# A hybrid decoder layer in float32: the 512 moving columns of the wide matmuls taken in turns from their two halves

## The chip, the core and the metric

The kernel runs on one core of one Trainium2 chip. The metric is the device time of one execution in microseconds. TensorE is called PE below, its weight load PEld, VectorE DVE, ScalarE ACT, GpSimd POOL, and SyncE, which issues the transfers, SP.

## The reference

One layer on 256 tokens of width 2048: a SwiGLU half-step, a token mixer of two branches side by side, and a second SwiGLU half-step, each between two RMS norms.

```python
h = rmsnorm(x, ffn1_norm_pre)
x = x + 0.5 * rmsnorm(swiglu(h, w_gate, w_up, w_down), ffn1_norm_post)   # 2048 -> 5632 -> 2048
h = rmsnorm(x, mix_norm_pre)
proj = h @ w_in                                   # 2048 -> 13376 columns, split in nine
y_a = mla_branch(c_q, c_kv, k_rope, ...)          # latent attention, 16 heads, then @ mla_w_o
y_b = hgrn2_branch(hq, hf, hi, hg, ...)           # gated linear recurrence, 16 heads, then @ hgrn_w_o
y = (sigmoid(gate_a) * y_a + sigmoid(gate_b) * y_b) @ w_out
x = x + rmsnorm(y, mix_norm_post)
...                                               # and the second SwiGLU half-step as the first
def swiglu(h, w_gate, w_up, w_down):
    return (jax.nn.silu(h @ w_gate) * (h @ w_up)) @ w_down
```

Nearly all of the work is in these products of a [256, K] activation with a weight matrix, and all weights are read once.

## The kernel before

**Operands.** Every float32 operand of a large product is held as an exact sum of two float32r parts, called hi and lo. An activation lies in SBUF transposed, as [feature in 128 partitions, part, k-tile, token], so that for one k-tile the 256 columns of hi and the 256 columns of lo are two runs of 256 with a gap between them (`act(k)`, a view of 128 x 2 x 256). A weight tile of 128 x 1024 is loaded by SP into `raw` (L83, four buffers), copied to hi by ACT (L95) and subtracted by DVE to give lo (L96). The product leaves out lo times lo.

**Two shapes of product.** `gemm_t` makes 256 weight columns at a time, with the weights stationary. For each k-tile and each half of the 256 columns it issues two matmuls into one PSUM bank of 512 columns: the weights' lo with the 256 hi columns of the activation as moving columns (L114, which adds into columns 0 to 255 of the bank), and the weights' hi with all 512, hi and lo (L115, which adds into all 512). In the first k-tile the wide one comes first (L111, then L112). The two halves of the bank are added at the end (L120 and L121). `gemm_n` makes 512 weight columns, with the activation stationary and 512 weight columns moving, and issues three matmuls for each k-tile and each half of the tokens through `_tok`: L126 (activation hi, weight hi), L127 (activation hi, weight lo), L128 (activation lo, weight hi), all into the same 512 columns.

**Stages.** Each half-step computes its first 512 columns of gate and up with `gemm_n`, then twenty rounds of a gate product (L295, `pg`) and an up product (L299, `pu`) with `gemm_t`, and then the down product with `closing`, which calls `gemm_n` for three quarters of the columns (L238) and once more, in another order of the tokens, for the fourth. The mixer calls `gemm_t` for the two gates (`gate_a`, `gate_b`), for the two output projections (`mla_w_o` with the tile `oa`, `hgrn_w_o` with the tile `ob`), and for q and f of the recurrence; `w_out` is again a `closing`. Tiles are named by use: `h` and `after` are the normed activations, `at` the SwiGLU product, `mg` the merged branches; `whi` and `wlo` are the split weights, `wpair` the split weights of a pass that are kept for the second half of the tokens.

**Order.** Each engine runs a fixed list of instructions. PE's list has the two matmuls of `gemm_t` by turns and the three of `gemm_n` in a row, with few other things between them in the stages named here.

Of the kernel before, what the change touches and what calls it, by code (L numbers as in the profile page):

```python
# [19 lines left out]
P = 128  # L20
# [3 lines left out]
KD = D // P  # L24
# [13 lines left out]
# Where the next operand's transposes stand in program order, along the product that runs beside them (see gemm_n), and  # L38
# by how many instructions the rest of that operand's chain is put ahead; columns of the residual at a time.
# [9 lines left out]
def _two_pi_parts():  # L49
    """2 pi as a sum of four 12-bit numbers and a rest."""  # L50
    parts, rest = [], TWO_PI
    for _ in range(4):
        step = 2.0 ** (np.floor(np.log2(rest)) - 11)
        c = np.floor(rest / step) * step
        parts.append(float(c))
        rest -= c
    parts.append(float(np.float32(rest)))
    return parts


class Ops:
    """Pools and the pieces that the stages share."""
# [36 lines left out]
    def gemm_t(self, w, act, kt):  # L99
        """256 weight columns, result transposed: a bank for 128 columns, [column, token] in two addends."""  # L100
        nc = self.nc
        ps = self.mm.tile([P, 2, 512], F32, name="mm")
        for g in range(kt // 4):
            hi, lo = self.load_w(w[g])
            for i in range(4):
                k = g * 4 + i
                for j in range(2):
                    c = slice(i * 256 + j * P, i * 256 + (j + 1) * P)
                    both = act(k)
                    if k == 0:  # L110
                        nc.tensor.matmul(ps[:, j], hi[:, c], both, start=True, stop=False)  # L111
                        nc.tensor.matmul(ps[:, j, 0:T], lo[:, c], both[:, 0], start=False, stop=False)  # L112
                    else:
                        nc.tensor.matmul(ps[:, j, 0:T], lo[:, c], both[:, 0], start=False, stop=False)  # L114
                        nc.tensor.matmul(ps[:, j], hi[:, c], both, start=False, stop=k == kt - 1)  # L115
        return ps

    def total(self, out, ps):
        """The sum of gemm_t's two addends."""
        self.nc.scalar.copy(out=out, in_=ps[:, :, T:512])  # L120
        self.nc.vector.tensor_tensor(out=out, in0=out, in1=ps[:, :, 0:T], op=ALU.add)  # L121

    def _tok(self, ps, hi, lo, act, k, kt, i, n, tt):
        nc = self.nc
        r, c, both, o = slice(tt * P, (tt + 1) * P), slice(i * n, (i + 1) * n), act(k), ps[tt][:, 0:n]
        nc.tensor.matmul(o, both[:, 0, r], hi[:, c], start=k == 0, stop=False)  # L126
        nc.tensor.matmul(o, both[:, 0, r], lo[:, c], start=False, stop=False)  # L127
        nc.tensor.matmul(o, both[:, 1, r], hi[:, c], start=False, stop=k == kt - 1)  # L128

    def gemm_n(self, w, act, kt, n=512, late=0, pool=None, own=0, hooks=()):  # L130
        """n weight columns, result [token, column], a bank for each half of the tokens.

        The first half of the tokens ends its last `late` k-tiles before the second half starts them. Their
        weights are in `pool`, but for the first `own` tiles. `hooks` are functions to call at points that run
        from -1 to 0 along the first half of the tokens, and from 0 to 1 along the second's last k-tiles."""
        kg = 1024 // n
        banks = self.mm.tile([P, 2, 512], F32, name="mm")
        ps = [banks[:, 0], self.mm.tile([P, 2, 512], F32, name="mm")[:, 1] if late else banks[:, 1]]
        held = []
        hooks = list(hooks)  # L140

        def call(at):
            while hooks and hooks[0][0] <= at:
                hooks.pop(0)[1](ps)

        for g in range(kt // kg):
            hold = g * kg >= kt - late
            hi, lo = self.load_w(w[g], pool if hold and g * kg >= kt - late + own * kg else None)
            call(g * kg / kt - 1)
            for i in range(kg):  # L150
                k = g * kg + i
                self._tok(ps, hi, lo, act, k, kt, i, n, 0)
                if hold:
                    held.append((hi, lo, k, i))
                else:
                    self._tok(ps, hi, lo, act, k, kt, i, n, 1)
        for m, (hi, lo, k, i) in enumerate(held):
            call(m / len(held))
            self._tok(ps, hi, lo, act, k, kt, i, n, 1)
        call(1)  # L160
        return ps if late else banks
# [10 lines left out]
    def rstd_of(self, ssq, n, width, half=False):  # L172
        """ssq [P, n] sums of squares -> 1 / sqrt(mean + eps), or half of it."""
# [20 lines left out]
    def transposed(self, src, act, c, tt):  # L194
        """split(transpose(src)) into the k-tiles 4c.. of act."""
# [10 lines left out]
    def prenorm(self, x, ssq, wname, act, tt, ws=None):  # L206
        """act = split(transpose(x * rstd * w)) for half of the tokens."""
# [10 lines left out]
    def weighted(self, ps, c, z, wname):  # L218
        """z = y * w, a quarter of the columns."""
        w = self.bcast(wname, c)  # L220
        self.nc.vector.tensor_tensor(out=z[:, c * 512:(c + 1) * 512], in0=ps, in1=w, op=ALU.mult)

    def residual(self, x, z, rstd, done):
        """x += rstd * z, some of the columns at a time."""
# [6 lines left out]
    def closing(self, w, act, kt, late, own, pool, post, half, x_src, x_dst, nxt):  # L231
        """The last product of a stage, its norm, the residual, and the next stage's operand.

        Returns the hooks of the next product, which end the operand."""
        z = [pool.tile([P, D], F32, name=f"z{tt}") for tt in range(NT)]
        yssq = [self.ssq4() for _ in range(NT)]
        for c in range(3):
            ps = self.gemm_n(w[c], act, kt)  # L238
            for tt in range(NT):
                self.square_sum(yssq[tt][:, c:c + 1], ps[:, tt])  # L240
                self.weighted(ps[:, tt], c, z[tt], post)
# [26 lines left out]
def layer_kernel(ctx, tc, a, out):  # L268
# [9 lines left out]
    def ffn(n, act, fp, x_src, x_dst, nxt, hooks=()):  # L278
# [3 lines left out]
        # the first columns by halves of the tokens  # L282
# [8 lines left out]
        for c in range((FF - FF_N) // 256):  # L291
            pg = ops.gemm_t(wg[c], act, KD)
# [3 lines left out]
            pu = ops.gemm_t(wu[c], act, KD)  # L296
# [48 lines left out]
    def gate_b(c):  # L345
        pg = ops.gemm_t(a["w_gb"][c], h, KD)
# [8 lines left out]
    for c in range(8):  # L355
        py = ops.gemm_t(a["mla_w_o"][c], lambda k: oa[:, :, k, :], KD)
# [9 lines left out]
    with tc.tile_pool(name="mg", bufs=1, side="right", reuse_waits="tile") as mgp:  # L366
        mg = mgp.tile([P, 2, KD, T], F32R, name="mg")
        for c in range(8):
            if c < 6:
                gts.append(gate_b(c + 2))  # L370
            py = ops.gemm_t(a["hgrn_w_o"][c], lambda k: ob[:, :, k, :], KD)
# [19 lines left out]
def rope_tables(ops, pool):  # L391
    """cos and sin of positions * inv_freq as [token, half of the tokens, HALF]."""
# [17 lines left out]
    # whole turns off: their number in parts of ten bits, so that each product with a part of 2 pi is exact  # L410
# [22 lines left out]
def mla(ops, mp, c_q, hm, h, oa, gate):  # L433
# [16 lines left out]
    def rope(dst, src, tt, n):  # L450
        """src [P, n, 64] -> dst, rotated."""
# [18 lines left out]
    # k_rope: product transposed, back to [token, dim], rotated, transposed, for the even and the odd  # L470
    # head of a pair in its half of the partitions, with zeros in the other
# [52 lines left out]
    def scores(pair, qn, kn, v):  # L524
        """The weights of a pair of heads, and what is left to do with them."""
# [46 lines left out]
    # a pair's projections, the weights of the pair before, and the output of that one later on  # L572
# [26 lines left out]
def hgrn(ops, gp, h, ob, fill):  # L599
# [8 lines left out]
    # lower bound: first row of the softmax over the two rows of logits  # L608
# [14 lines left out]
    def pair_in(pr, step):  # L623
        """q, f, k as [feature, half of the tokens, head, token]; the second half runs back in time."""
# [28 lines left out]
    def values_in(g):  # L653
        """Values of four heads, [token, half of the tokens, head and feature]."""
# [5 lines left out]
    def gates_in(g):  # L660
        """Their output gates, with the norm's weights."""
# [11 lines left out]
    def scan(pr, q, f, k, four):  # L673
        """pre: products of f within blocks up to and with t; suf: products after s to the end of the block.

        Scores of pairs (s, t) in the two halves of a block of 2n tokens are k suf . q pre with blocks of n. In
        the second half of the tokens time runs back, so that there an earlier s has the place of a later
        one in the first half: one product gives both."""
# [7 lines left out]
        def part(t, n, early):  # L686
            """The earlier (or later) halves of the blocks of 2n: [P, half of the tokens, block, n]."""
# [3 lines left out]
        def ends(t, n, early):  # L691
            """The last element in time of those halves, over n columns."""
# [3 lines left out]
        def halves(t, n, tt, early):  # L696
            """The same as part, of one half of the tokens: [P, block, n]."""
# [93 lines left out]
    # a pair's products, the scores of the one before, and the output of the one before that  # L791
# [33 lines left out]
def _tiles(w, cols, group):  # L825
    """[K, C] -> [C / cols, K / (group * 128), 128, group * cols]"""
# [6 lines left out]
def _tokens(x):  # L833
    """Tokens in the kernel's order: the second half runs back in time."""
# [64 lines left out]
```

## Time and profile before

| | before |
|---|---|
| two timed runs, us | 2564.88 and 2566.22, median 2565.55 |
| the profiled execution's own time, first to last instruction, us | 2564.2 |
| PE busy, us | 2521.4 (98%) |
| weight loads busy, us | 2147.1 (84%) |
| DVE, ACT, POOL busy, us | 1477.7, 1186.9, 181.1 |
| mean granted TensorE clock | 0.999 |
| read from HBM, MB | 472.61 |

The profile has no other time of the profiled execution than its span, which is 1.35 us below the median of the timed runs. Matmuls overlap in the pipeline, and the end of each is modelled, so that a row's duration (393 ns for a matmul of 512 columns) is longer than the time that the matmul takes from its neighbours. What one matmul costs is read from the distance of the starts in the timeline.

### The profile page before, as it was taken

To read this page: it belongs to the slowest core of one execution; us is meant where nothing else is said; L and a number is where in the kernel's file an instruction comes from. 1 tells how busy PE (TensorE), PEld (TensorE's weight loads), DVE (VectorE), ACT (ScalarE), POOL (GpSimd) and SP (SyncE) were. 2 spreads that over 40 slices of the span, in tenths; PEclk is the share of its full clock that TensorE was granted. 3 is DMA by queue.
4 is the path that set the end of the run, shared out by engine and by line. 5 is a ranking of instruction groups with operands and counts; after the bars stand their busy time and mean duration, and the time that the engine had idled before them with its cause. 6 is when DMAs were issued, how large, how long until landed. Compare 5 with 4: busy or idle time off the path is not lost.

```text
span 2564.2 us, 33907 instructions
## 1 busy us (share of the span) xinstructions
PE 2521.4 (98%) x13316; PEld 2147.1 (84%) x13316; DVE 1477.7 (58%) x1732; ACT 1186.9 (46%) x1552; POOL 181.1 (7%) x181
## 2 busy tenths in 40 slices
PE   8999999999999999999999999999999999999998
PEld 6888888888878898888888888888788888888887
DVE  5555555544466666556777776555655555554444
ACT  5444444434344556444444444444544444443433
POOL 0000000000000100111323231120000000000000
PEclk9999999999999999999999999999999999999999
DMA  7555555556686444555545444567755555555655
GB/s 255 174 188 189 188 183 190 188 188 199 201 271 188 162 140 148 188 181 181 165 163 169 161 157 158 188 205 242 231 175 188 187 186 188 189 189 188 197 195 184
DMA packets 137248, 481.13 MB, mean 188 GB/s; under 512 B 15616, under 2 KB 16000, under 8 KB 136320
## 3 DMA queue, kind: packets, MB, share of 16 engines
q1 hardware_dynamic: 137088, 478.97, 57.3%
q8 instruction: 104, 1.70, 0.3%
q14 instruction: 56, 0.46, 0.1%
HBM read 472.61 MB, written 6.29 MB: 187 GB/s over the span
## 4 chain that ended last, share of the span: by engine, by line
PE 93%; DVE 3%; POOL 1%; issue 1%; DMA 1%; ACT 1%; SPq 0%; POOLq 0%; DVEq 0%; ACTq 0%
PE mm L115 34%; PE mm L114 18%; PE mm L126 11%; PE mm L127 11%; PE mm L128 11%; PE mm L111 2%; PE mm L112 1%; POOL suf L706 1%; PE tp L198 0%; DVE sT L711 0%; PE sp L534 0%; PE sp L533 0%; DVE wlo L96 0%; PE sp L728 0%; PE tp L565 0%
## 5 line engine op out<-in xcount | busy, mean ns | idle before, releaser
L96 DVE TENSOR_TENSOR wlo<-raw,whi 128x1024 fp32r<-128x1024 f32 x826 | 1024.8, 1243 | 763.5 <-ACT whi L95 762.3
L95 ACT CAST whi<-raw 128x1024 fp32r<-128x1024 f32 x826 | 865.7, 1050 | 891.2 <-PE mm L115 425.3
L115 PE MATMUL mm<-h,whi 128*128 128x512 f32 x2400 | 846.0, 393 | 0.0
L114 PE MATMUL mm<-h,wlo 128*128 128x256 f32 x2400 | 678.1, 283 | 0.0
L115 PEld LDWEIGHTS mm<-h,whi 128*128 128x128 f32 x2400 | 450.7, 188 | 100.7
L114 PEld LDWEIGHTS mm<-h,wlo 128*128 128x128 f32 x2400 | 451.2, 188 | 3.8
L115 PE MATMUL mm<-after,whi 128*128 128x512 f32 x960 | 340.1, 394 | 0.0
L114 PE MATMUL mm<-after,wlo 128*128 128x256 f32 x960 | 273.1, 284 | 0.0
L127 PE MATMUL mm<-wlo,at 128*128 128x512 f32 x664 | 262.0, 395 | 0.0
L126 PE MATMUL mm<-whi,at 128*128 128x512 f32 x664 | 262.0, 395 | 0.0
L128 PE MATMUL mm<-whi,at 128*128 128x512 f32 x664 | 261.7, 395 | 0.0
L115 PEld LDWEIGHTS mm<-after,whi 128*128 128x128 f32 x960 | 180.4, 188 | 38.9
L114 PEld LDWEIGHTS mm<-after,wlo 128*128 128x128 f32 x960 | 180.6, 188 | 1.2
L126 PEld LDWEIGHTS mm<-whi,at 128*128 128x128 f32 x664 | 125.1, 188 | 29.2
L128 PEld LDWEIGHTS mm<-whi,at 128*128 128x128 f32 x664 | 125.1, 188 | 29.2
L127 PEld LDWEIGHTS mm<-wlo,at 128*128 128x128 f32 x664 | 125.1, 188 | 29.2
L178 POOL TENSOR_TENSOR rs<-ms,mhalf 128x1 f32<-128x1 f32 x16 | 9.7, 605 | 1633.3 <-DVE ms L176 1633.3
L126 PE MATMUL mm<-whi,after 128*128 128x512 f32 x304 | 120.9, 398 | 1.2 <-ACT after L164 1.2
L128 PE MATMUL mm<-whi,after 128*128 128x512 f32 x304 | 120.1, 395 | 0.0
L127 PE MATMUL mm<-wlo,after 128*128 128x512 f32 x304 | 120.0, 395 | 0.0
L115 PE MATMUL mm<-oa,whi 128*128 128x512 f32 x240 | 84.6, 393 | 0.0
L115 PE MATMUL mm<-ob,whi 128*128 128x512 f32 x240 | 84.6, 393 | 0.0
(276 smaller groups left out, 2860.9 us busy)
## 6 DMA issues: line engine op xcount, KB each, us to landing
raw<-in_ffn_w_gate SPq DMA_DIRECT2D x176, 512.0 KB, 4.3
raw<-in_ffn_w_up SPq DMA_DIRECT2D x176, 512.0 KB, 3.5
raw<-in_ffn_w_down SPq DMA_DIRECT2D x176, 512.0 KB, 4.3
raw<-in_w_ga SPq DMA_DIRECT2D x32, 512.0 KB, 3.4
raw<-in_mla_w_o SPq DMA_DIRECT2D x32, 512.0 KB, 3.6
raw<-in_w_hq SPq DMA_DIRECT2D x32, 512.0 KB, 3.6
raw<-in_w_hf SPq DMA_DIRECT2D x32, 512.0 KB, 3.5
raw<-in_w_hi SPq DMA_DIRECT2D x32, 512.0 KB, 3.5
```

The costliest lines, as they stand in the source:

```text
L95: nc.scalar.copy(out=hi, in_=raw)
L96: nc.vector.tensor_tensor(out=lo, in0=raw, in1=hi.bitcast(F32), op=ALU.subtract)
L111: nc.tensor.matmul(ps[:, j], hi[:, c], both, start=True, stop=False)
L112: nc.tensor.matmul(ps[:, j, 0:T], lo[:, c], both[:, 0], start=False, stop=False)
L114: nc.tensor.matmul(ps[:, j, 0:T], lo[:, c], both[:, 0], start=False, stop=False)
L115: nc.tensor.matmul(ps[:, j], hi[:, c], both, start=False, stop=k == kt - 1)
L126: nc.tensor.matmul(o, both[:, 0, r], hi[:, c], start=k == 0, stop=False)
L127: nc.tensor.matmul(o, both[:, 0, r], lo[:, c], start=False, stop=False)
L128: nc.tensor.matmul(o, both[:, 1, r], hi[:, c], start=False, stop=k == kt - 1)
L178: self.nc.gpsimd.tensor_tensor(out=r, in0=ms, in1=self.mhalf[:, 0:n], op=ALU.pow)
L706: G.tensor_tensor(out=part(suf, n, True), in0=part(suf, n, True), in1=ends(pre, n, False), op=ALU.mult)
```

## The change

Matmuls of 512 moving columns take a parameter e. With e set, the 512 columns are seen as two halves of 256, and both the moving operand and the PSUM output are read and written in another order: e columns of the first half, e of the second, the next e of the first, and so on. Each column still goes to the place that it went to, so that the sums in PSUM are the same. Only L115 of `gemm_t` (the halves are the activation's hi and lo) and L127 of `gemm_n` (the halves are the first and the last 256 of 512 weight columns) are so changed, and only in some calls. The rest keeps the order that it had, with e left at None.

| where | e | matmuls | line of the changed kernel |
|---|---|---|---|
| up product of the first half-step | 2 | 600 | L113 |
| up product of the second half-step | 4 | 600 | L115 |
| the three `closing` stages, first quarter of the columns | 4 | 176 + 32 | L115 |
| `mla_w_o` | 8 | 240 | L117 |
| `hgrn_w_o` | 16 | 240 | L119 |
| gate product of the first half-step | 32 | 600 | L121 |
| the three `closing` stages, second quarter | 32 | 176 + 32 | L121 |
| `gate_b` | 64 | 240 | L123 |
| gate product of the second half-step | 128 | 600 | L125 |
| the three `closing` stages, third quarter | 128 | 176 + 32 | L125 |

These are 3744 matmuls in all. The seven branches of `wide` all issue the same call; they give each e a line of its own. Comments and docstrings are gone too.

```diff
+    def turned(self, o, moving, e):
+        if len(moving.shape) == 2:
+            moving = moving.rearrange("p (s n) -> p s n", s=2)
+        return (o.rearrange("p (s c e) -> p c s e", s=2, e=e), moving.rearrange("p s (c e) -> p c s e", e=e))
+
+    def wide(self, e, o, w, moving, **flags):
+        mm = self.nc.tensor.matmul
+        if e is None:
+            mm(o, w, moving, **flags)
+            return
+        o, moving = self.turned(o, moving, e)
+        if e == 2:
+            mm(o, w, moving, **flags)
+        elif e == 4:
+            mm(o, w, moving, **flags)
...
+        else:
+            mm(o, w, moving, **flags)
 
-    def gemm_t(self, w, act, kt):
+    def gemm_t(self, w, act, kt, e=None):
...
                         nc.tensor.matmul(ps[:, j, 0:T], lo[:, c], both[:, 0], start=False, stop=False)
-                        nc.tensor.matmul(ps[:, j], hi[:, c], both, start=False, stop=k == kt - 1)
+                        self.wide(e, ps[:, j], hi[:, c], both, start=False, stop=k == kt - 1)
...
-    def _tok(self, ps, hi, lo, act, k, kt, i, n, tt):
+    def _tok(self, ps, hi, lo, act, k, kt, i, n, tt, e=None):
...
-        nc.tensor.matmul(o, both[:, 0, r], lo[:, c], start=False, stop=False)
+        self.wide(e, o, both[:, 0, r], lo[:, c], start=False, stop=False)
...
-            ps = self.gemm_n(w[c], act, kt)
+            ps = self.gemm_n(w[c], act, kt, e=(4, 32, 128)[c])
...
-            pg = ops.gemm_t(wg[c], act, KD)
+            pg = ops.gemm_t(wg[c], act, KD, 32 if n == 1 else 128)
...
-            pu = ops.gemm_t(wu[c], act, KD)
+            pu = ops.gemm_t(wu[c], act, KD, 2 if n == 1 else 4)
...
-        pg = ops.gemm_t(a["w_gb"][c], h, KD)
+        pg = ops.gemm_t(a["w_gb"][c], h, KD, 64)
...
-        py = ops.gemm_t(a["mla_w_o"][c], lambda k: oa[:, :, k, :], KD)
+        py = ops.gemm_t(a["mla_w_o"][c], lambda k: oa[:, :, k, :], KD, 8)
...
-            py = ops.gemm_t(a["hgrn_w_o"][c], lambda k: ob[:, :, k, :], KD)
+            py = ops.gemm_t(a["hgrn_w_o"][c], lambda k: ob[:, :, k, :], KD, 16)
```

On PE, in an up product of the first half-step, the list of before reads as follows (the tile `h_86` is the normed activation, `mm` the PSUM tile; the last numbers are partitions and columns):

```order
1200 L114 MATMUL mm<-h_86,wlo 128x256
1201 L115 MATMUL mm<-h_86,whi 128x512
1202 L114 MATMUL mm<-h_86,wlo 128x256
1203 L115 MATMUL mm<-h_86,whi 128x512
1204 L114 MATMUL mm<-h_86,wlo 128x256
1205 L115 MATMUL mm<-h_86,whi 128x512
```

and that of the change, at the same place:

```order
1200 L142 MATMUL mm<-h_86,wlo 128x256
1201 L113 MATMUL mm<-h_86,whi 128x128x2x2
1202 L142 MATMUL mm<-h_86,wlo 128x256
1203 L113 MATMUL mm<-h_86,whi 128x128x2x2
1204 L142 MATMUL mm<-h_86,wlo 128x256
1205 L113 MATMUL mm<-h_86,whi 128x128x2x2
```

Nothing has moved: the narrow matmul has another line number, and the wide one's 512 columns have become 128 turns of 2 halves of 2 columns.

On PE, in the first quarter of the first half-step's down product, before:

```order
2878 L127 MATMUL mm<-wlo,at 128x512
2879 L128 MATMUL mm<-whi,at 128x512
2880 L126 MATMUL mm<-whi,at 128x512
2881 L127 MATMUL mm<-wlo,at 128x512
2882 L128 MATMUL mm<-whi,at 128x512
```

and with the change:

```order
2878 L115 MATMUL mm<-wlo,at 128x64x2x4
2879 L156 MATMUL mm<-whi,at 128x512
2880 L154 MATMUL mm<-whi,at 128x512
2881 L115 MATMUL mm<-wlo,at 128x64x2x4
2882 L156 MATMUL mm<-whi,at 128x512
```

Here too every row stands where it stood; one matmul of three has a new order of its columns, 64 turns of 2 halves of 4. PE's list has 12826 rows before and after, and apart from line numbers and these column orders the two are alike, as are the lists of DVE, ACT, POOL and SP.

More of the change, by code (lines that the diff above doesn't have):

```diff
@@ L97, in load_w @@
         return hi, lo
-    def gemm_t(self, w, act, kt):
+    def turned(self, o, moving, e):
[12 more added lines that the diff above has]
+            mm(o, w, moving, **flags)
+        elif e == 8:
+            mm(o, w, moving, **flags)
+        elif e == 16:
+            mm(o, w, moving, **flags)
+        elif e == 32:
+            mm(o, w, moving, **flags)
+        elif e == 64:
+            mm(o, w, moving, **flags)
+        else:
+            mm(o, w, moving, **flags)
+    def gemm_t(self, w, act, kt, e=None):
         nc = self.nc
@@ L126, in _tok, with gemm_n @@
         nc.tensor.matmul(o, both[:, 0, r], hi[:, c], start=k == 0, stop=False)
-        nc.tensor.matmul(o, both[:, 0, r], lo[:, c], start=False, stop=False)
+        self.wide(e, o, both[:, 0, r], lo[:, c], start=False, stop=False)
         nc.tensor.matmul(o, both[:, 1, r], hi[:, c], start=False, stop=k == kt - 1)
-    def gemm_n(self, w, act, kt, n=512, late=0, pool=None, own=0, hooks=()):
+    def gemm_n(self, w, act, kt, n=512, late=0, pool=None, own=0, hooks=(), e=None):
         kg = 1024 // n
@@ L151, in gemm_n @@
                 k = g * kg + i
-                self._tok(ps, hi, lo, act, k, kt, i, n, 0)
+                self._tok(ps, hi, lo, act, k, kt, i, n, 0, e)
                 if hold:
@@ L155, in gemm_n @@
                 else:
-                    self._tok(ps, hi, lo, act, k, kt, i, n, 1)
+                    self._tok(ps, hi, lo, act, k, kt, i, n, 1, e)
         for m, (hi, lo, k, i) in enumerate(held):
             call(m / len(held))
-            self._tok(ps, hi, lo, act, k, kt, i, n, 1)
+            self._tok(ps, hi, lo, act, k, kt, i, n, 1, e)
         call(1)
```

## The prediction

> **What bounds the kernel now.** I read the page's busy shares first, then the chain that ended last, then stretches of the stages that the change touches, and last the distances between matmul starts in the timeline.
>
> ```profile
> span 2564.2 us, 33907 instructions
> PE 2521.4 (98%) x13316; PEld 2147.1 (84%) x13316; DVE 1477.7 (58%) x1732; ACT 1186.9 (46%) x1552; POOL 181.1 (7%) x181
> PEclk9999999999999999999999999999999999999999
> PE 93%; DVE 3%; POOL 1%; issue 1%; DMA 1%; ACT 1%; SPq 0%; POOLq 0%; DVEq 0%; ACTq 0%
> ```
>
> PE is busy for 98% of the span, at full granted clock in each of the 40 slices, and 93% of the chain that ended last is PE's own. A busy PE can still be one that waits inside an instruction, so the next view is one by stage: the gate and up products of the two half-steps.
>
> ```profile
> core 0: us, PE busy (x) PEld busy (x) DVE busy (x) ACT busy (x) POOL busy (x), PEclk, DMA share, GB/s
> 100.00:500.00 400.00, 400.00 (x2281) 350.22 (x2280) 221.05 (x215) 187.63 (x214) 0.00 (x0) 1.00 0.58 188
> 1880.00:2300.00 420.00, 420.00 (x2394) 367.78 (x2393) 231.70 (x225) 195.93 (x224) 0.00 (x0) 1.00 0.58 188
> ```
>
> PE has no idle time at all in these stretches. DVE is busy for 221 of 400 us, ACT for 188, the transfers use 0.58 of their engines. So in these stages each nanosecond that a matmul gains or loses goes to the end of the program: nothing waits beside PE that could hide a loss, and up to 40% of slack in the engines that feed it lets a gain through. The waits of PE are all outside: its longest sum is 16.4 us, of the transposes between stages.
>
> ```profile
> PE tp L198 <- DVE xn L214: 16.4, 5, 9.7
> ```
>
> **What one matmul costs.** The durations are modelled and overlap, so I take distances of starts. The first two rows below are seven turns of a narrow and a wide matmul apart in an up product, where the timeline has these two alternately.
>
> ```profile
> 399.71 0.40 PE L115 MATMUL mm<-h,whi 128*128 128x512 f32 x1
> 399.94 0.28 PE L114 MATMUL mm<-h,wlo 128*128 128x256 f32 x1
> 400.06 0.40 PE L115 MATMUL mm<-h,whi 128*128 128x512 f32 x1
> ...
> 402.17 0.40 PE L115 MATMUL mm<-h,whi 128*128 128x512 f32 x1
> ```
>
> From 399.71 to 402.17 is 2.46 us for 7 turns, or 351 ns a turn. The narrow one takes 0.12 (from 399.94 to 400.06), so the wide one takes some 231 ns. The same for 35 matmuls of 512 contiguous columns in the first down product:
>
> ```profile
> 659.75 0.39 PE L126 MATMUL mm<-whi,at 128*128 128x512 f32 x1
> ...
> 667.88 0.39 PE L128 MATMUL mm<-whi,at 128*128 128x512 f32 x1
> ```
>
> 8.13 us for 35, or 232 ns each, which is 0.453 ns a column. The kept weights of the same product, 29 steps at one place later, are a little faster:
>
> ```profile
> 742.00 0.39 PE L126 MATMUL mm<-wpair,at 128*128 128x512 f32 x1
> ...
> 748.58 0.39 PE L128 MATMUL mm<-wpair,at 128*128 128x512 f32 x1
> ```
>
> 6.58 us for 29, or 227 ns. These are the same shapes with the moving columns at another place in SBUF. So where the columns lie is worth 5 ns of a wide matmul, and no wide matmul in these rows takes under 227.
>
> **The change part by part.** It removes no instruction, adds none, and moves none on any engine. The transfers and the waits are those of before. The first k-tiles (L111), the last quarter of each down product and all calls with e at None are as they were. What it changes is the order of the columns in 3744 wide matmuls, and the price is that of a jump from one half to the other. A matmul with blocks of e has 512/e blocks and so about as many jumps:
>
> - e = 2: 256 jumps, 600 matmuls, 153,600
> - e = 4: 128 jumps, 808 matmuls, 103,424
> - e = 8: 64 jumps, 240 matmuls, 15,360
> - e = 16: 32 jumps, 240 matmuls, 7,680
> - e = 32: 16 jumps, 808 matmuls, 12,928
> - e = 64: 8 jumps, 240 matmuls, 1,920
> - e = 128: 4 jumps, 808 matmuls, 3,232
>
> That is 298,144 jumps, 86% of them in e = 2 and 4. The counts of matmuls come from these groups, with their first k-tiles apart (600 is a quarter of the 2400):
>
> ```profile
> L115 PE MATMUL mm<-h,whi x2400: 387/396/400, 66.2 to 2310.5; 128*128 128x512 f32 x185
> L115 PE MATMUL mm<-oa,whi x240: 387/396/400, 1031.4 to 1120.2; 128*128 128x512 f32 x120
> L115 PE MATMUL mm<-ob,whi x240: 387/396/400, 1571.3 to 1716.3; 128*128 128x512 f32 x120
> L127 PE MATMUL mm<-wlo,at x664: 387/393/404, 515.0 to 2548.6; 128*128 128x512 f32 x166
> L127 PE MATMUL mm<-wlo,mg x108: 393/394/398, 1716.7 to 1798.5; 128*128 128x512 f32 x108
> ```
>
> **The price of a jump** is not in the trace for PE at short runs, so I bound it from the nearest rows. The first is L115 itself: its moving operand already has one gap, between hi and lo, and its 231 ns stand beside 232 for the contiguous L126 to L128. One jump on the read side costs at most a nanosecond or so, and may cost nothing. The second is DVE's product in the recurrence, which reads and writes runs of 1, 2, 4, 8, 16, 32 and 64 columns in SBUF by turns, eight times each:
>
> ```profile
> L707 DVE TENSOR_TENSOR f<-f x56: 415/425/428, 1151.0 to 1549.3; 128x256 f32<-128x256 f32 x56
> ```
>
> All 56 lie between 415 and 428 ns. Between runs of 1 and runs of 64 there are some 250 jumps of difference, so a jump costs DVE at most 13/250 = 0.05 ns. This row is far off in two ways: DVE takes more than a nanosecond a column where PE takes 0.453, and it writes SBUF and not PSUM. At DVE's bound the whole change would cost 298,144 x 0.05 = 15 us. From below: no reason excludes that the turns let the columns come as smoothly as at the best place seen, 227 ns; that would save 3744 x 5 ns = 19 us. The upper end is a jump that costs a whole column's time, 0.453 ns; that is 135 us, and it is a rival below. Between these ends I take zero. The row of DVE shows addresses that turn between short runs without a cost, the row of L115 shows a gap without a cost, and 2 columns of 4 bytes are the shortest run, so that neighbours always come in pairs. **Sum:** span 2564.2 + 0 = 2564.2 us, and with the 1.35 us by which the median of the timed runs lies above the profiled span, 2565.6, or 2566 us. The likeliest case's own range is 2565.6 - 19 to 2565.6 + 15, or 2547 to 2581.
>
> The Trainium skill has a rule that speaks against this. Its page "PSUM — Partial Sum Buffer", under Specifications (TRN2), gives 8-byte lines and says that any non-contiguous access pattern slows matmuls significantly. It names no figure; the first rival is what it would do here. The page "SBUF — State Buffer", under Specifications (TRN2), has 16-byte lines, asks for two hits on a line for the full rate, and has each crossing to a new line pay; a run of 2 columns just meets the first, and by that the sum stays as it is. The trace can't judge between the two: every matmul in it writes contiguous columns.
>
> **Rivals.**
>
> *Each jump costs PE column time, on its read or on its write.* At a whole column, 0.453 ns: e = 2 loses 70 us, e = 4 47, all others together 19; the sum is 135 us and the time 2565.6 + 135 = 2701 us. At half of that, one lost column for every two jumps, 68 us and 2633 us. For it speaks that a PE column is more than twice as fast as DVE's, that PE writes PSUM, which no short run in the trace does, and that 227 against 232 ns shows PE to feel where its columns lie. Against it speak L115's gap and DVE's flat row. Since nothing hides a loss here, it decides from 2% of the time, 51 us over 298,144 jumps, or 0.17 ns a jump: a good third of a column. The prices are those of the rows; the rule of the PSUM page gives the mechanism a name.
>
> *A run of 2 columns takes as long to fetch as a run of 4.* Then only e = 2 loses, and its wide matmuls take twice 232 ns: 600 x 232 = 139 us and 2705 us. For it speaks that the first half-step's up product is the only place with such runs, so that no other row excludes it; against it that DVE's runs of 2 (415 to 428 with all others) show no such step.
>
> *The turns are better than the two long runs.* If the 5 ns between 232 and 227 went, the time would be 2565.6 - 19 = 2547 us, still within 2%. To be faster by 2% each of the 3744 matmuls would have to lose 51,300/3744 = 14 ns, to 218 ns, 9 ns under any place that these rows show.
>
> *The change does not do what it says.* If the patterns were put together again before the chip sees them, the time would be 2566 too; the lists of instructions show 128x128x2x2 in the place of 128x512, so this has next to no chance.
>
> **How the numbers follow.** No cost, or one within the likeliest range: 0.56, with the small gains in it. Column time for jumps, in full or in part: 0.28, from 2617 (the 2% line) to 2701. Runs of 2 at half rate: 0.13, 2705. A gain beyond 2%: 0.03. The predicted time is that of the first, 2566 us. The chances are faster 0.03, same 0.56, slower 0.41; a difference of 2% is about what a measurement of this kernel can tell from none. The range takes in the likeliest case from 2550 and the first rival nearly up to its full price, to 2695; what is left out is the full price of the two rivals above that and the gains below.
>
> **What would show it.** The changed kernel has a line for each e, so the distances of starts on L113 (e = 2) beside L125 (e = 128) tell the price of a jump at once: 231 on both if I am right; 231 + 256 x 0.453 = 347 on L113, 289 on L115 and 233 on L125 by the first rival; 464 on L113 and 231 on L115 by the second. The stages keep their places if I am right: L115's first matmul on `oa` at 1031 us and on `ob` at 1571 us. If `oa` starts later by 70 us or more while the stretch between `oa` and `ob` keeps its 540 us, the loss is in short runs. I would be wrong in the reading of what bounds the kernel if the distances grew and the span did not.

## The result, and the profile after

The changed kernel takes 2657.11 us, the median of two runs (2655.75 to 2658.47), against 2565.55 before: a ratio of 1.0357 with a 95% interval from 1.0327 to 1.0388. It is slower. The range on record, 2550 to 2695, holds the time; its likeliest case, no difference with a range of its own from 2547 to 2581, did not come true.

The profile's page after, with the span, the busy engines, the granted clock and the engines' shares of the chain that ended last:

```profile
span 2656.7 us, 33909 instructions
PE 2613.8 (98%) x13316; PEld 2155.2 (81%) x13316; DVE 1477.7 (56%) x1732; ACT 1190.4 (45%) x1552; POOL 180.8 (7%) x181
PEclk9999999999999999999999999999999999999999
PE 94%; DVE 2%; POOL 1%; issue 1%; DMA 1%; ACT 1%; SPq 0%; POOLq 0%; DVEq 0%; ACTq 0%
```

The span is 92.5 us longer and PE is busy for 92.4 us more (2613.8 - 2521.4). Number of matmuls, work of DVE and granted clock are as before. So the time went into PE instructions that take longer, and not into waits. The waits of PE confirm it: the longest sum was 16.4 us before and is now 16.0.

```profile
PE tp L226 <- DVE xn L242: 16.0, 5, 9.8
```

The distances of starts in an up product of the first half-step (e = 2), ten turns of narrow and wide from the first row to the last:

```profile
390.87 0.50 PE L113 MATMUL mm<-h,whi 128*128 128x512 f32 x1
391.19 0.29 PE L142 MATMUL mm<-h,wlo 128*128 128x256 f32 x1
391.32 0.49 PE L113 MATMUL mm<-h,whi 128*128 128x512 f32 x1
...
395.38 0.51 PE L113 MATMUL mm<-h,whi 128*128 128x512 f32 x1
```

4.51 us for ten turns, or 451 ns where it was 351. The gate product of the second half-step (e = 128), ten turns too:

```profile
1959.62 0.39 PE L125 MATMUL mm<-h,whi 128*128 128x512 f32 x1
...
1963.13 0.40 PE L125 MATMUL mm<-h,whi 128*128 128x512 f32 x1
```

3.51 us, 351 ns a turn: nothing has changed there. The groups by line, with the modelled duration (minimum, median, maximum in ns) and the first and last start in us, show the same order; before, the median was 396 for L115 of `gemm_t` and 393 for L127 on `at`.

```profile
L113 PE MATMUL mm<-h,whi x600: 487/492/508, 77.5 to 579.6; 128*128 128x512 f32 x150
L115 PE MATMUL mm<-h,whi x600: 409/423/431, 1946.5 to 2400.7; 128*128 128x512 f32 x150
L117 PE MATMUL mm<-oa,whi x240: 402/407/408, 1099.5 to 1190.7; 128*128 128x512 f32 x120
L119 PE MATMUL mm<-ob,whi x240: 400/400/404, 1641.7 to 1788.7; 128*128 128x512 f32 x120
L121 PE MATMUL mm<-h,whi x600: 398/401/407, 66.1 to 565.4; 128*128 128x512 f32 x150
L125 PE MATMUL mm<-h,whi x600: 387/396/400, 1935.3 to 2388.6; 128*128 128x512 f32 x150
```

PE's list is the same before and after, so each matmul can be set beside its counterpart. Below are the mean distances from its start to the next matmul's start.

| e, line, tile | matmuls | before, ns | after, ns | sum, us |
|---|---|---|---|---|
| 2, L113, h | 600 | 230.7 | 325.4 | 56.8 |
| 4, L115, h | 600 | 230.7 | 258.6 | 16.7 |
| 4, L115, at and mg | 208 | 232.5 | 249.0 | 3.5 |
| 8, L117, oa | 240 | 230.7 | 241.7 | 2.7 |
| 16, L119, ob | 240 | 230.7 | 237.1 | 1.5 |
| 32, L121, h | 600 | 230.7 | 239.8 | 5.5 |
| 32, L121, at | 176 | 232.2 | 235.6 | 0.6 |
| 64, L123, and 128, L125 | 1048 | | | under 0.3 |
| narrow ones beside them, L142, h | 2400 | 120.2 | 121.7 | 3.5 |

These rows make 91 of the 92.5 us. More than half is e = 2, in one product of the first half-step, and the loss of the narrow matmuls stands there too: those between two of L113 went from 120.4 to 126.3 ns, the other narrow ones on `h` stayed within 1 ns.

### The profile page after: what moved, and what is told of

It reads as the page before. It is cut to its first block, busy times and chain, and to the rows that moved or that the text cites. A ratio compares the mean times of both kernels' runs of the same rounds, so it can differ in the third digit from the quotient of the medians.

```text
span 2656.7 us, 33909 instructions
## 1 busy us (share of the span) xinstructions
PE 2613.8 (98%) x13316; PEld 2155.2 (81%) x13316; DVE 1477.7 (56%) x1732; ACT 1190.4 (45%) x1552; POOL 180.8 (7%) x181
## 4 chain that ended last, share of the span: by engine, by line
PE 94%; DVE 2%; POOL 1%; issue 1%; DMA 1%; ACT 1%; SPq 0%; POOLq 0%; DVEq 0%; ACTq 0%
PE mm L142 17%; PE mm L109 12%; PE mm L154 11%; PE mm L156 11%; PE mm L115 8%; PE mm L113 8%; PE mm L121 7%; PE mm L125 7%; PE mm L139 2%; PE mm L117 2%; PE mm L119 2%; PE mm L123 2%; PE mm L140 1%; POOL suf L734 1%; PE tp L226 1%
## 5 line engine op out<-in xcount | busy, mean ns | idle before, releaser
L142 PE MATMUL mm<-h,wlo 128*128 128x256 f32 x2400 | 682.9, 285 | 0.0
L142 PEld LDWEIGHTS mm<-h,wlo 128*128 128x128 f32 x2400 | 452.9, 189 | 3.5
L142 PE MATMUL mm<-after,wlo 128*128 128x256 f32 x960 | 272.9, 284 | 0.0
L113 PE MATMUL mm<-h,whi 128*128 128x512 f32 x600 | 271.9, 495 | 0.0
L156 PE MATMUL mm<-whi,at 128*128 128x512 f32 x664 | 262.3, 396 | 0.0
L109 PE MATMUL mm<-after,whi 128*128 128x512 f32 x720 | 254.8, 394 | 0.0
L115 PE MATMUL mm<-h,whi 128*128 128x512 f32 x600 | 228.5, 423 | 0.0
L121 PE MATMUL mm<-h,whi 128*128 128x512 f32 x600 | 216.6, 402 | 0.0
L125 PE MATMUL mm<-h,whi 128*128 128x512 f32 x600 | 211.5, 393 | 0.0
L113 PEld LDWEIGHTS mm<-h,whi 128*128 128x128 f32 x600 | 117.2, 195 | 80.0
L142 PEld LDWEIGHTS mm<-after,wlo 128*128 128x128 f32 x960 | 180.6, 188 | 1.2
L109 PEld LDWEIGHTS mm<-after,whi 128*128 128x128 f32 x720 | 135.3, 188 | 29.3
L156 PEld LDWEIGHTS mm<-whi,at 128*128 128x128 f32 x664 | 124.7, 188 | 29.9
L115 PEld LDWEIGHTS mm<-h,whi 128*128 128x128 f32 x600 | 113.5, 189 | 40.3
L121 PEld LDWEIGHTS mm<-h,whi 128*128 128x128 f32 x600 | 112.7, 188 | 29.3
L125 PEld LDWEIGHTS mm<-h,whi 128*128 128x128 f32 x600 | 112.7, 188 | 25.2
L154 PE MATMUL mm<-whi,after 128*128 128x512 f32 x304 | 120.9, 398 | 1.3 <-ACT after L192 1.3
```

The source lines that it names most:

```text
L109: mm(o, w, moving, **flags)
L113: mm(o, w, moving, **flags)
L115: mm(o, w, moving, **flags)
L121: mm(o, w, moving, **flags)
L125: mm(o, w, moving, **flags)
```

## The experiments

All changes below are to the changed kernel, unless the kernel before is named. Where no number of runs is given, a time is that of a single execution.

**Read or write (e1, e2).** Two theories were open: short runs cost where the moving operand is read from SBUF, or where the result is written to PSUM. Each kernel turns one side alone.

```diff
-        o, moving = self.turned(o, moving, e)
+        _, moving = self.turned(o, moving, e)      # e1
+        o, _ = self.turned(o, moving, e)           # e2
```

> Only the moving operand is read by turns; PSUM is written in the order of its columns, so that this kernel's sums land in the wrong columns and its output isn't the reference's. Theory R, the short runs cost on the read of the moving operand: the starts stand as in the changed kernel, some 325 ns on L113 (e = 2), 259 on L115 (e = 4, up product), 240 on L121 (e = 32), and the span is 2657 us. Theory W, they cost on the write into PSUM: 231 to 232 ns on every line and a span of 2564 us. A mixture shows as a part on each side.

> Only PSUM is written by turns; the moving operand is read as before the change, so that this kernel's sums land in the wrong columns and its output isn't the reference's. Theory R: 231 to 232 ns on every line, span 2564 us. Theory W: 325 ns on L113, 259 on L115, 240 on L121, span 2657 us. If the two sides each cost and the slower one hides the other, this run and the one with the read alone both lie above 2564 and add up to more than 92 us.

2657.76 us with the read turned, 2566.93 with the write turned, and 2564.84 to 2566.94 for the runs of the kernel before beside them. The span and the groups of the first, then of the second:

```profile
span 2656.0 us, 33907 instructions
L113 PE MATMUL mm<-h,whi x600: 488/492/508, 77.9 to 579.9; 128*128 128x512 f32 x150
L115 PE MATMUL mm<-h,whi x600: 409/423/431, 1945.6 to 2399.8; 128*128 128x512 f32 x150
```

```profile
span 2565.2 us, 33909 instructions
L113 PE MATMUL mm<-h,whi x600: 387/396/400, 78.0 to 515.0; 128*128 128x512 f32 x150
L115 PE MATMUL mm<-h,whi x600: 387/396/400, 1874.5 to 2311.5; 128*128 128x512 f32 x150
```

The read alone carries the whole loss, down to the distances of each line (325.4, 258.6, 239.8 ns again). The write in runs of 2 to 128 columns, two halves in turns, costs nothing: 396 is the median of before, and the mean distances on `h` are 230.7 ns at e = 2, 4, 32 and 128 alike. The theory of the write is out.

**The value of e, or the place (e3).** In the change each e has a place of its own, and e = 32 (9 ns more) costs more than e = 16 (6 ns). The seven values change places.

```diff
-            pg = ops.gemm_t(wg[c], act, KD, 32 if n == 1 else 128)
+            pg = ops.gemm_t(wg[c], act, KD, 2 if n == 1 else 16)
-            pu = ops.gemm_t(wu[c], act, KD, 2 if n == 1 else 4)
+            pu = ops.gemm_t(wu[c], act, KD, 32 if n == 1 else 8)
...
-            ps = self.gemm_n(w[c], act, kt, e=(4, 32, 128)[c])
+            ps = self.gemm_n(w[c], act, kt, e=(2, 8, 16)[c])
```

`mla_w_o`, `hgrn_w_o` and `gate_b` get 4, 64 and 128.

> The same seven values of e in other places: 2 in the first half-step's gate product, 32 in its up product, 16 and 8 in those of the second half-step, 4 in mla_w_o, 64 in hgrn_w_o, 128 in gate_b, and 2, 8, 16 in the closing stages. If the price hangs on e alone: 325 ns on L113 in the gate product, 240 on L121 in the up product, 259 on L115 with the tile oa, 241 and 237 on L117 and L119, a span near 2660 us. If the 9 ns of e = 32, which is more than the 6 ns of e = 16, came from the place and not from e, L121 falls to 231 here and L113 or L119 carries it.

2678.63 us; mean distances 325.5 ns for e = 2 (now the gate product), 239.8 for e = 32 (now the up product), 262.8 for 4 on `oa`, 242.8 for 8, 236.9 for 16. On `at`, e = 2 takes 320.1. The price goes with e in the main. The place has a part in the small prices: e = 4 takes 258.6 on `h`, 262.8 on `oa` and 249.2 on `at`, and e = 32 costs more than 16 in `gemm_t` (239.8 against 236.9) but less on `at` (235.6 against 238.3). The total is 19 us above what I expected, mostly because the 208 matmuls of e = 2 in the closing stages cost nearly as much each as those of `gemm_t` (18 us in all) and the line behind them (L156 on `at`) lost 3 us in all, and because with e = 4 on `oa` the narrow matmuls beside them went from 120 to 131.

**Do the lines add up (e4).** e = 2 and 4 back to None.

```diff
-            pu = ops.gemm_t(wu[c], act, KD, 2 if n == 1 else 4)
+            pu = ops.gemm_t(wu[c], act, KD)
-            ps = self.gemm_n(w[c], act, kt, e=(4, 32, 128)[c])
+            ps = self.gemm_n(w[c], act, kt, e=(None, 32, 128)[c])
```

> e = 2 and e = 4 back to None, all else as in the change. If the loss is the sum of what the lines show: 56.8 + 16.7 + 3.5 us go away with the wide matmuls and up to 3.5 more with the narrow ones between them, span 2576 to 2580 us, a ratio of 1.005 to 1.006 to the kernel before. If something besides the wide matmuls' own spacing were lost (waits, transfers), the rest would be larger.

2577.33 us, the median of four runs, a ratio of 1.0045 (1.0029 to 1.0062) to the kernel before. The profiled span is 2575.1 us, 81.6 below that of the change, and the wide and narrow rows had promised 77 to 80.5. So the loss is the matmuls' own time, but for about 1 us.

**Length of the run, or distance of the hop (e5).** The closing stages alone, with nine orders, read and write alike: halves 1 KB apart taken in turns (as in the change), and orders that sweep over the columns with a short hop, such as columns 0, 1, 4, 5, 8, 9 and so on, and in a second sweep 2, 3, 6, 7 and so on. Below is one line of the code for each three orders; the numbers in brackets are those of the other two.

```diff
+    def turned(self, x, s, e):
+        return x.rearrange("p (s c e) -> p c s e", s=s, e=e)
+            mm(t(o, 2, 8), w, t(moving, 2, 8), **flags)         # L107, L109 (2, 2), L111 (2, 4)
+            mm(t(o, 128, 2), w, t(moving, 128, 2), **flags)     # L113, L115 (16, 2), L117 (64, 4)
+            mm(t(o, 32, 8), w, t(moving, 32, 8), **flags)       # L119, L121 (4, 2), L123 (16, 4)
```

> Only the first three quarters of the closing stages have turned orders, here on all three lines of a product, read and write alike, so that the sums are the same; the products with stationary weights are as before the change. Halves 1 KB apart: blocks of 8, 2 and 4 on L107, L109, L111. Blocks of 2 with a hop of 16 bytes (L113), 128 (L115) and 512 (L121); blocks of 4 with a hop of 32 bytes (L117) and 128 (L123); blocks of 8 with a hop of 64 bytes (L119). Theory run: the price hangs on the length of the run alone; some 320 ns on L109, L113, L115, L121, 249 on L111, L117, L123, 242 on L107 and L119. Theory hop: it hangs on the distance, as if far places collided; then the near hops, L113, L117 and L119, stand near 232 and the others as far as their distance goes.

2740.61 us. The timeline where L109, L111 and L107 follow each other, where L117, L113 and L115 do, and where L123, L119 and L121 do:

```profile
540.86 0.50 PE L109 MATMUL mm<-wlo,at 128*128 128x512 f32 x1
541.19 0.41 PE L111 MATMUL mm<-whi,at 128*128 128x512 f32 x1
541.43 0.41 PE L107 MATMUL mm<-whi,at 128*128 128x512 f32 x1
...
625.10 0.41 PE L117 MATMUL mm<-whi,at 128*128 128x512 f32 x1
625.35 0.61 PE L113 MATMUL mm<-whi,at 128*128 128x512 f32 x1
625.79 0.65 PE L115 MATMUL mm<-wlo,at 128*128 128x512 f32 x1
626.25 0.41 PE L117 MATMUL mm<-whi,at 128*128 128x512 f32 x1
...
720.22 0.43 PE L123 MATMUL mm<-whi,at 128*128 128x512 f32 x1
720.49 0.40 PE L119 MATMUL mm<-whi,at 128*128 128x512 f32 x1
720.72 0.64 PE L121 MATMUL mm<-wlo,at 128*128 128x512 f32 x1
721.18 0.43 PE L123 MATMUL mm<-whi,at 128*128 128x512 f32 x1
```

Runs of 2 take 434 ns with a hop of 16 bytes (L113), 467 with 128 (L115) and 460 with 512 (L121), but 327 where two halves take turns (L109). Runs of 4 take 249 to 266, runs of 8 take 244 in turns and 233 with a hop of 64 bytes. The theory of the hop is out: it had L113, with the shortest hop, near 232. My theory of the run had the right order but not the numbers: 320 is not the price of runs of 2, and L119 takes 233 where it had 242. Runs of 2 in a sweep take about twice the straight time, and in turns with one other half something is saved. No run writes these sweeps into PSUM without reading them too; e9 sets the read apart.

**Lines of 16 bytes (e9).** That doubling suggests that PE fetches the moving operand in lines of 4 columns and pays for the line, used or not. Then it is not the run that counts but the boundaries that it crosses. The same nine orders, with the weights 8 bytes into their tiles; the writes into PSUM are those of e5:

```diff
-            hi = self.wp.tile([P, 1024], F32R, name="whi", bufs=4)
+            hi = self.wp.tile([P, 1032], F32R, name="whi", bufs=4)[:, 2:1026]
```

(and `wlo` likewise).

> The run with nine orders in the closing stages, with one difference: the split weights start 8 bytes (two columns) into their tiles, so that they are off the 16-byte boundaries that they kept so far. Theory line: the moving operand is fetched in aligned lines of 16 bytes (4 columns), each for the time of 4 columns whether 2 or 4 of them are used. Then a run of 4 now touches two lines: L117 (4, hop 32 bytes) goes from 252 to some 434 ns, L123 (4, hop 128) from 266 to some 460, L111 (4, halves 1 KB apart) from 249 towards 327; a run of 8 touches three lines in place of two and L119 goes from 233 to some 325; runs of 2 stay: L113 434, L109 327. Theory run: the price hangs on how many columns follow each other, wherever they start; every line stays within a few ns.

2882.32 us. The timeline of the same lines:

```profile
540.68 0.50 PE L111 MATMUL mm<-whi,at 128*128 128x512 f32 x1
541.01 0.52 PE L107 MATMUL mm<-whi,at 128*128 128x512 f32 x1
...
624.72 0.63 PE L113 MATMUL mm<-whi,at 128*128 128x512 f32 x1
625.17 0.64 PE L115 MATMUL mm<-wlo,at 128*128 128x512 f32 x1
625.63 0.63 PE L117 MATMUL mm<-whi,at 128*128 128x512 f32 x1
626.08 0.63 PE L113 MATMUL mm<-whi,at 128*128 128x512 f32 x1
...
759.47 0.64 PE L123 MATMUL mm<-whi,at 128*128 128x512 f32 x1
759.91 0.52 PE L119 MATMUL mm<-whi,at 128*128 128x512 f32 x1
760.26 0.64 PE L121 MATMUL mm<-wlo,at 128*128 128x512 f32 x1
```

| order | lines visited, e5 and e9 | e5, ns | e9, ns |
|---|---|---|---|
| 4, hop 32 bytes (L117) | 128, 256 | 252 | 452 |
| 4, hop 128 bytes (L123) | 128, 256 | 266 | 447 |
| 8, hop 64 bytes (L119) | 128, 192 | 233 | 348 |
| 2, hop 16 bytes (L113) | 256, 256 | 434 | 453 |
| 4, halves in turns (L111) | 128, 256 | 249 | 329 |
| 8, halves in turns (L107) | 128, 192 | 244 | 353 |
| 2, halves in turns (L109) | 256, 256 | 327 | 334 |

512 straight columns touch 128 lines in 227 ns, or 1.77 ns a line. 256 lines at that rate are 454 ns and 192 are 340: the rows L117, L123 and L119 land within 2.5% of it, with the same run lengths as in e5 (for L119 I had expected some 325 ns and not 348). The theory of the run, which had them stay, is out. L109 and L111 save over a quarter of 454. In both, a line's second half is wanted again after one block of the other half, which is one line in L109 and two in L111 off its boundary. With three lines between, nothing is saved: L121, four parts in turns, takes 460 ns where 454 is the full price, and L107 off its boundary 353 where it is 340. That the nearness of the second visit saves the time is read from these four rows; no run varies it alone.

**Larger pieces (e6, e7).** All tiles lie 32 bytes past a multiple of 64. A tile of 32 bytes ahead of them removes that, in the changed kernel and in the kernel before.

```diff
+        self.pad = self.const.tile([P, 8], F32, name="pad")
         self.ident = self.const.tile([P, P], F32, name="ident")
```

> The change with one more tile of 32 bytes ahead of all others, so that each operand starts at a multiple of 64 bytes and not 32 past one. Theory pieces: the moving operand is fetched in aligned pieces of 64 bytes (16 columns), and a block that straddles two costs an extra step; then e = 16 and e = 32 fall to what e = 128 has (231 ns), e = 8 stays near 240, e = 4 and 2 stay, and the span falls by some 8 us to 2648. Theory run: nothing in the alignment, 2657 us, 237 and 240 ns on L119 and L121 as before.

> The kernel before with the same 32 bytes ahead. Theory pieces: a run of 512 columns that starts off a multiple of 64 bytes touches 33 pieces in place of 32, so wide matmuls gain a few ns at most (231 to some 225), up to 40 us over some 8000 wide ones. Theory run: 2564 us, nothing.

2659.54 and 2565.85 us; the distances are as without the pad (e = 16: 237.2 ns, e = 32: 239.8), but for the 32 matmuls of e = 4 on `mg` (242.8 for 248.2). Aligned pieces of 64 bytes do not explain the small prices.

**The place in SBUF (e8, e10, e11).** The prediction had seen 227 beside 232 ns for the same shape at another place. Two kernels move tiles of the kernel before.

```diff
-        self.wp = ctx.enter_context(tc.tile_pool(name="wp", bufs=1))
...
         self.hp = ctx.enter_context(tc.tile_pool(name="hp", bufs=1))
+        self.wp = ctx.enter_context(tc.tile_pool(name="wp", bufs=1))
```

> The kernel before with the pool of the normed activations ahead of that of the weights in SBUF, so that whi and wlo lie 32 KB higher and the activations 40 to 50 KB lower. It asks why the kept weights (wpair) run at 227 ns and whi and wlo at 232. If the place of the moving tile sets it, the spacing of L115 or of L126 to L128 changes here by some ns, and the span by up to 50 us either way. If it is something else in that pass, 2564 us and 231 to 232 ns.

> The kernel before with the pool of the normed activations ahead of the weights' pool, once more and timed: one look gave 2551 us. If that look was typical, a ratio of 0.994 to 0.995 with an interval below 1, down products at 227 ns a matmul, pairs at 353. If it was chance, a ratio of 1.

2551.39 us, and 2551.59 as the median of five timed runs, a ratio of 0.9945 (0.9931 to 0.9959): faster than both kernels of this case. `whi` and `wlo` as moving operands now run at 227 ns in the down products:

```profile
655.05 0.39 PE L126 MATMUL mm<-whi,at 128*128 128x512 f32 x1
655.28 0.39 PE L127 MATMUL mm<-wlo,at 128*128 128x512 f32 x1
655.51 0.39 PE L128 MATMUL mm<-whi,at 128*128 128x512 f32 x1
655.74 0.39 PE L126 MATMUL mm<-whi,at 128*128 128x512 f32 x1
```

The products with moving `h` lost 5 ns on the wide matmul (236) and won 3 on the narrow one (117). From that I made a rule, that the lower 64 KB are the slow place, and put weights (`wlo` as `whi` below) and activations both at the upper end:

```diff
-        self.hp = ctx.enter_context(tc.tile_pool(name="hp", bufs=1))
+        self.hp = ctx.enter_context(tc.tile_pool(name="hp", bufs=1, side="right"))
+        self.wr = ctx.enter_context(tc.tile_pool(name="wr", bufs=1, side="right"))
...
-            hi = self.wp.tile([P, 1024], F32R, name="whi", bufs=4)
+            hi = self.wr.tile([P, 1024], F32R, name="whi", bufs=4)
```

> The kernel before with the split weights and the normed activations at the upper end of SBUF (whi and wlo from 192 KB, h from 160 KB) and all else below; orders of columns as before the change. Theory place: a wide matmul costs some 5 ns more where its moving or its stationary tile lies in the lower 64 KB (whi moving there 232, above it 227; h moving there 236). Then the pair of a narrow and a wide matmul falls from 351 towards 340 ns, the down products to 227, and the span by 40 to 60 us to 2505 to 2525 us. Theory neighbour: it is the distance between the two tiles, or what else lies near them, that counts; then the sum may go either way, and 2564 us with pairs of 351 ns is as likely as 2551.

2563.34 us, the median of eleven runs, a ratio of 0.9989 (0.998 to 0.9998): not the 2505 to 2525 of the rule. The narrow and the wide matmul with moving `h` together take 353 ns, not the 340 of the rule. `whi` runs at 226 to 228 ns beside `mg` and the mixer's activations and at 233 beside `at`, in the same upper place. So the rule is wrong, and the moving tile's place alone does not set the time. Whether the other operand's place does, or what else runs in that stage, is not shown.

## Why the prediction was right and wrong

- *What bounds the kernel* was right. PE has no slack in these stages, and the loss in the matmuls (91 us in the table) is the loss of the span (92.5).
- *The change moves nothing, and only the order of columns can cost* was right: PE's busy time took all of it, and the waits stayed.
- *The price of a jump, "Between these ends I take zero"*, is the step that failed. The ends were a saving of 19 us and a loss of 135; the loss was 92.5. The reason for zero was DVE's flat row: 415 to 428 ns for 256 columns in runs of 1 to 64. It could not carry that. At 425/256 = 1.66 ns a column, its fixed part included, DVE takes 3.3 ns for a run of 2, longer than the 1.77 ns of a line (e5, e9), so that a half-used line would not show there. That is argued and not shown: no run has DVE's price of a line, and PE's 1.77 ns for each of 256 runs of one column would make 453 ns, more than the 428 that DVE took at most. For PE it is shown (e1, e5, e9): straight columns use a whole line each 1.77 ns, and a line of which half is used is time lost.
- *"neighbours always come in pairs"* was the other reason, and it is wrong for the same cause: on PE's read it takes four, starting on a line.
- *The first rival*, a fixed price for each jump, gave 68 to 135 us and brackets the result, but not by its mechanism. The price per jump is 94.7/256 = 0.37 ns at e = 2, 0.22 at 4, 0.17 at 8, 0.20 at 16, 0.57 at 32 and nothing at 64 and 128. Its other side, the write into PSUM, costs nothing (e2). The range on record holds the time because it was drawn to take in nearly all of this rival. Its jumps have no fixed price, so that the range holds by luck and not because its mechanism was right.
- *The second rival*, a run of 2 takes as long to fetch as a run of 4, names the mechanism (e9 shows it), with two sizes off. It had 464 ns on L113 and 325.4 was measured, since the turns between two halves save a part; and it had 231 on L115 and e = 4 to 32 without a loss, which together cost 30.5 us, a third of the whole. For e = 4 to 32, all lines are used in full, so that the line alone does not explain these 3 to 28 ns a matmul; what does was not found.
- *What would show it* worked nearly as written: L113 far from L125, `oa` later by 68 us where 70 or more was named (1099.5 against 1031.4), and 542 us from `oa` to `ob` where it was 540.

## What to carry to other kernels

Before an operand's order is changed for a PE-bound product, look at which side is turned: here the write to PSUM took runs of 2 columns for nothing, while the float32r moving operand wants whole aligned lines of 16 bytes, best one after the other, and in turns between two halves only runs of 64 columns or more were free. Count lines and not runs: a block of 4 that starts 8 bytes off costs as much a column as one of 2. And don't bound an engine's price by a row of an engine that takes nearly four times as long for each column.

## What the runs showed of the hardware

- A float32r matmul of 512 straight columns takes 227 to 232 ns. If each of its 128 lines of 16 bytes costs what a line costs in e9, where 256 took 447 to 453 ns, it is at the limit of the fetch of its moving operand; that is an estimate from these rows. Half-used lines in a sweep took 434 to 467 ns in e5.
- A half-used line is partly spared if its other half is read after one other line (327 ns) or two (329), and not after three (460).
- Writes into PSUM in runs of 2, 4, 8, 16 and 32 columns, two halves in turns, are free (2566.93 against 2565.39 us). The Trainium skill, "PSUM — Partial Sum Buffer", Specifications (TRN2), has any non-contiguous pattern slow matmuls significantly. This case's measurement decides against that for such turns of 2 columns or more; single columns were not measured.
- The Trainium skill, "SBUF — State Buffer", Specifications (TRN2), has 16-byte lines, asks for two hits on a line for the full rate, and has each crossing to a new line pay. e9 agrees with the lines. It does not agree with the two hits: two hits of float32r take 434 to 467 ns and four take 227 to 266. Paying for each new line fits e9, where twice the lines took twice the time; the prediction named it too, but went by the two hits alone.
- The same matmul takes 227 or 232 ns by where tiles lie in SBUF (e8, e11), and that layout of the kernel before won 0.55%. The rule behind it was not found.
